# A hybrid Conformer/RWKV-7 step: recurrence steps and square sums traced next to the low-rank and block products

## The chip, the cores and the metric

The kernel runs on one core of one Trainium2 chip. The metric is the device time of one launch in microseconds; the kernel before took 2652.4 us, the median of three runs (2649.21, 2652.4 and 2652.9).

## The reference, cut to what matters

Two layers are applied to 1040 prompt tokens (16 learned ones and 1024 of the prompt) and to 8 single tokens that continue stored states. Layer 0 mixes with a causal convolution, layer 1 with RWKV-7; each is followed by a squared-ReLU MLP. The change touches layer 1's mixer alone:

```
r = xr @ w_r;  k = xk @ w_k;  v = xv @ w_v
w_log = -softplus(-(w0 + tanh(xw @ w1) @ w2)) - 0.5
decay = exp(-exp(w_log))
a = sigmoid(a0 + (xa @ a1) @ a2)
g = sigmoid(xg @ g1) @ g2
kk = k * k_k, divided by its norm in each head
k = k * (1 + (a - 1) * k_a)
# scan over tokens, S: 64 x 64 in each of 16 heads
sa = S @ -kk_t
S = S * w_t + outer(sa, kk_t * a_t) + outer(v_t, k_t)
y = S @ r_t
bonus = sum(r * k * r_k) * v
out = ((groupnorm(y) + bonus) * g) @ w_o
```

The scan over single tokens is computed in 17 chunks (16 tokens, then 16 times 64) with products of small matrices and the inverse of a triangular matrix in each chunk.

## The kernel before, in words

**Stages.** Layer 0 comes first, then layer 1's mixer input (about 1000 to 1715 us of the profiled execution), then layer 1's output projection, its MLP and the last norm. In the mixer input the tokens go through in four groups (`G1`, 272, 256, 256 and 264 columns; called group 0 to 3 here), and within a group in eight blocks `p` of 128 channels. The tokens of groups 0 to 3 make chunks 0 to 4, 5 to 8, 9 to 12 and 13 to 16.

**One block `p` of a group** (`mixer_in`) traces these products for TensorE, in this order: the `r` projection (`proj`, eight 128x128 weight blocks, tile `pr`); for p over 2 one block of the next group's `k` projection (`keys`, tile `pk`); the low-rank products `l_g` (full array) and `l_w`, `l_a` (64 rows of the array each, side by side); the `v` projection (`pv`); then for the block before it (`finish`, whose `trace` is called one block late through `late`) the transposes `vt`, the block products `nn` (64x32 parts of the array) and the bonus sum `pk<-rk`; and at last `pb`, which spreads the key norms. ScalarE takes `l_w` and `l_a` through two tanh and two copies (L1131, L1132), then `am`, `em` and `ex` (L1159, L1146, L1150); VectorE scans the decay (L1143) and makes the chunk's operands `ab`.

**The square sums.** Each block of `k` is squared on ScalarE (`sq`, L948) and its per-head sums are four products into the tile `pn` (L939, 128x32 parts of the array). Before the change those of a block follow the next `k` block's projection (`add_pn`).

**The recurrence** trails one group behind. `tick` lets it advance: `advance` adds `PACE` (1.4, 1.3, 2.4 in groups 1 to 3) to a credit and runs pieces of the generator `chunk` while the credit is positive; each piece costs its entry of `RW`. A chunk's pieces are: the products `A` in two halves (`front`, tiles `A`, 64x128 parts), `gg` (32x32 parts) with the transposes `bT`, `W` (128x64) with `po` (32x32), `U` (64x64), and `S` with `Y` (128x64). `norm_gate` adds transposes `yn`. `invert` advances the triangular inverses, which are VectorE work with a DMA on either side. Before the change a block calls `tick` five times through `both`: ahead of `r`, twice inside `r` (after weight blocks 2 and 5 of 8, `proj`'s `fill`) and twice inside `v`; a `k` block calls it twice more.

**What sets the order.** TensorE's order is the order of tracing (`tc.manual_schedule`). The other engines' orders are made by a scheduler from the dependencies, so they move when TensorE's order does. PSUM has four banks for the projections and the like (tag `mm`, used in turn), three for the recurrence (tag `w`) and one for `pn` (tag `x`). A product that needs a bank waits until what was in it has been read.

Of the kernel before, what the change touches and what calls it, by code (L numbers as in the profile page):

```python
# [8 lines left out]
F32 = mybir.dt.float32  # L9
# [7 lines left out]
P = 128  # L17
# [16 lines left out]
N1 = 272  # L34
# [12 lines left out]
def hybrid_step(tc, x_prompt, x_sample, state_conv, state_shift, state_wkv, meta_tokens,  # L47
# [10 lines left out]
    with ctx:  # L58
# [48 lines left out]
        for name, ap in vecs:  # L107
            n = ap.shape[0]
# [85 lines left out]
        def bank(name, tag="mm"):  # L194
            return cur[tag].tile([P, 512], F32, name=name, tag=tag)
# [200 lines left out]
        with ExitStack() as l0:  # L396
# [294 lines left out]
            with ExitStack() as s:  # L691
# [3 lines left out]
                fill, rest = filler(8 * KT, ([ranked(CV0, conv(0)), ranked(CV0, ln_silu(0))], EARLY * (15 * KT // 2 + 2 + 2 * MW + KT)))  # L695
# [4 lines left out]
                first = pw1_weights(0, 0)  # L700
# [5 lines left out]
                for g in range(3):  # L706
# [6 lines left out]
                    def both():  # L713
                        if g:
                            fill()
                        if g < 2:
                            nxt()
# [37 lines left out]
        for i, op in enumerate((ALU.is_gt, ALU.is_ge)):  # L755
            v = m_ar[:HS, i * HS:(i + 1) * HS]
# [75 lines left out]
        pr = pool(ld, "pr", 1)  # L832
# [86 lines left out]
        def proj(w, act, n, name, fill=None):  # L919
            ps = bank(f"p{name}")  # L920
            for k in range(KT):
                nc.tensor.matmul(ps[:, :n], w[:, k, :], act[k], start=k == 0, stop=k == KT - 1)  # L922
                if fill and k in (2, 5):
                    fill()
            return ps

        def keys(g, fill):

            c0, n = G1[g]
            nm = lambda s, *a: f"{s}{g}" + "".join(f"_{x}" for x in a)  # L930
            mix, _, act = prep[g]
            act = act or [mix(2, k) for k in range(KT)]
            pn = bank(nm("pn"), "x")
            add_pn = lambda: None

            def to_pn(p, sq):
                def add():
                    for j in range(4):
                        nc.tensor.matmul(pn[32 * j:32 * j + 32, :n // 4], head_sel(p), sq[:, n // 4 * j:n // 4 * (j + 1)],  # L939
                                         start=p == 0, stop=p == KT - 1, tile_position=(0, 32 * j))  # L940
                return add
            for p in range(KT):
                yield
                ps = proj(next(wrkv), act, n, nm("k", p), fill)
                k_ = kept[g, p] = pr.tile([P, N1], F32, name=nm("st", p), tag="st", bufs=KT + 1)
                nc.scalar.copy(k_[:, :n], ps[:, :n])
                sq = pr.tile([P, N1], F32, name=nm("sq", p), tag="rk", bufs=2)
                nc.scalar.activation(sq[:, :n], ps[:, :n], AF.Square, scale=vec("k_k", p))  # L948
                add_pn()
                add_pn = to_pn(p, sq)  # L950
            yield
            w = n // 4
            r16, low = (lorap.tile([P, N1 // 4], F32, name=nm("r16" + q), tag="lf", bufs=2)[:, :w] for q in "fl")
            high = lorap.tile([P, N1 // 4], F32R, name=nm("r16h"), tag="lh")[:, :w]
            norm[g] = lorap.tile([P, N1], F32R, name=nm("r16"), tag="r16", bufs=2)[:, :n]
            add_pn()
            nc.vector.tensor_scalar(r16, pn[:, :w], L2_EPS * L2_EPS, None, op0=ALU.max)
            nc.scalar.activation(r16, r16, AF.Sqrt)
            nc.vector.reciprocal(r16, r16)
# [7 lines left out]
        def mixer_in(g, tick):  # L967
# [63 lines left out]
            def t_(name, p, tag=None, bufs=1):  # L1031
                return pr.tile([P, N1], F32, name=nm(name, p), tag=tag or name, bufs=bufs)
# [19 lines left out]
                next(kend, None)  # L1052

            def finish(p, rk, ab, vv):
                def trace():
                    for s in segs:
                        if s[3] == HS:
                            nc.gpsimd.dma_start(d_ab[s[0], :, p].rearrange("c r i x -> r c (i x)"),
# [38 lines left out]
                    nc.gpsimd.dma_start(d_n[ch0:ch0 + ncg, p].rearrange("c r t -> r c t"), n32[:, :ncg])  # L1097
                    if g == 0:
                        nc.gpsimd.dma_start(d_n[0, p], n32[:, 4])
                    pb = bank(nm("pk", p))  # L1100
                    nc.tensor.matmul(pb[:, :n], hsum, rk[:, :n], start=True, stop=True)
                    bv = t_("bv", p)
# [1 line left out]
                    return lambda: nc.gpsimd.dma_start(d_bv[:, p, c0:c0 + n], bv[:, :n])  # L1104
                return trace

            late, later = (lambda: lambda: None), lambda: None
            for p in range(KT):
                both()
                ps = proj(next(wrkv), act, n, nm("r", p), both if p else first)  # L1110
                rk2 = pr.tile([P, 2, N1], F32, name=nm("rk2", p), tag="rk2", bufs=2)
                nc.scalar.copy(rk2[:, 1, :n], ps[:, :n])
                if p == 0:
# [13 lines left out]
                pls = [bank(nm("l2", f"{b}{p}")) for b in "wa"]  # L1127
                for i, pl in enumerate(pls):
                    nc.tensor.matmul(pl[:, :n], wa2[HALF[i], p, :], lwa[HALF[i], :n], start=True, stop=True, tile_position=(HS * i, 0))
                for pl, t, nb, sign in zip(pls, (cum, nav), ("w0", "a0"), (0.5, -0.5)):  # L1130
                    nc.scalar.activation(t[:, :n], pl[:, :n], AF.Tanh, scale=0.5, bias=hvec(nb, p))  # L1131
                    nc.scalar.activation(t[:, :n], t[:, :n], AF.Copy, scale=sign, bias=sign)  # L1132
                ps = proj(next(wrkv), act_v, n, nm("v", p), both)
                vv = t_("vv", p, "vv", 2)
                nc.scalar.copy(vv[:, :n], ps[:, :n])
                later()
                later = late()
                nkk, rp = (rk2[:, i, :] for i in range(2))
                kp = kept.pop((g, p))
                pb = bank(nm("pb", p))  # L1140
# [20 lines left out]
                bb, km = wa[:, 0, :], wa[:, 1, :]  # L1161
                nc.vector.tensor_mul(km[:, :n], kp[:, :n], am[:, :n])
                nc.vector.tensor_mul(bb[:, :n], nkk[:, :n], nav[:, :n])
                rk = t_("rk", p, "rk", 2)
                nc.vector.scalar_tensor_tensor(rk[:, :n], rp[:, :n], vec("r_k", p), km[:, :n], op0=ALU.mult, op1=ALU.mult)

                ab = pr.tile([P, 5, 4, HS], F32, name=nm("ab", p), tag="ab", bufs=2)
# [28 lines left out]

            def tail():
                later()
                late()()
                for c, k in ([(0, 1)] if g == 0 else []) + [(ch0, ncg)]:  # L1200
                    invs.append(inverses(c, k))
            carry["tail"] = tail
# [585 lines left out]
```

## Time and profile before

| | us |
|---|---|
| median of three runs | 2652.4 |
| the profiled execution | 2651.75 |
| its span, first to last instruction | 2649.8 |
| outside the span | 1.95 |
| TensorE busy in the span | 2594.1 |
| mean granted TensorE clock | 0.994 |

In the timeline of TensorE a row is a run of equal products: its start, its length up to the modelled end of the last one, and how many passes there are (an f32 product makes two). Since products overlap, the time that a run takes is the distance from its start to the next row's start. In front of the shapes stands the part of the array that the product uses, rows by columns: 128\*128 is all of it. Square brackets hold idle time in front of the row, with what ended it.

### The profile page before, as it was taken

How to read it: one execution, taken by the hardware profiler on the slowest of the kernel's cores; microseconds unless marked ns; L12 is line 12 of the kernel's file. 1: busy time of each engine (PE TensorE's matmuls, PEld its weight loads, DVE VectorE, ACT ScalarE, POOL GpSimd, SP SyncE). 2: the span in 40 equal slices, each digit the busy share in tenths (PEclk: the TensorE clock that was granted, in tenths of full speed). 3: DMA queues.
4: the chain of work that ended last, by engine and by line, in shares of the span. 5: the costliest groups of instructions: out<-in, count | busy, mean ns of one | idle time of the engine just before them, and what ended most of it. 6: DMA issues, size and time to landing. Idle time of an engine off the chain costs nothing.

```text
span 2649.8 us, 51719 instructions
## 1 busy us (share of the span) xinstructions
PE 2594.1 (98%) x19956; PEld 2432.9 (92%) x19956; DVE 1717.6 (65%) x3610; ACT 1128.8 (43%) x2093; POOL 1456.7 (55%) x2060
## 2 busy tenths in 40 slices
PE   9999999999999999999999999899999999999998
PEld 8999999999999999777777777789999999999998
DVE  6999999997444444445757567686679554444435
ACT  5546435444444333243344545545444542222223
POOL 7677878878878777022211113476588763333331
PEclk9999999999999999999999999999999999999999
DMA  7663544554446543677776867898575542222211
GB/s 190 172 168 108 167 141 133 160 172 137 138 138 187 155 136 112 191 211 202 214 184 181 213 160 194 218 207 195 142 219 174 153 132 65 72 68 69 72 48 44
DMA packets 602060, 400.24 MB, mean 151 GB/s; under 512 B 96128, under 2 KB 548928, under 8 KB 601814
## 3 DMA queue, kind: packets, MB, share of 16 engines
q1 hardware_dynamic: 573764, 360.08, 49.6%
q0 software_dynamic: 8720, 26.35, 3.0%
q10 hardware_dynamic: 19330, 10.49, 1.4%
q8 instruction: 158, 2.59, 0.4%
q14 instruction: 88, 0.72, 0.1%
HBM read 338.94 MB, written 58.83 MB: 150 GB/s over the span
## 4 chain that ended last, share of the span: by engine, by line
PE 85%; DVE 8%; ACT 2%; issue 2%; DMA 1%; POOL 1%; SPq 0%; ACTq 0%; DVEq 0%; POOLq 0%
PE ps_in L190 8%; PE ps_in L192 8%; PE ps_in L191 8%; PE out L190 8%; PE out L191 8%; PE out L192 8%; PE pk L922 4%; PE pr L922 4%; PE pv L922 3%; PE ps_g L190 1%; PE ps_o L192 1%; PE ps_g L191 1%; PE ps_g L192 1%; PE ps_oo L190 1%; PE ps_o L190 1%
## 5 line engine op out<-in xcount | busy, mean ns | idle before, releaser
L165 POOL TENSOR_TENSOR wo_lo<-wo_raw,wo_hi 128x256 fp32r<-128x256 f32 x736 | 543.0, 770 | 286.6 <-ACT wo_hi L158 279.2
L165 POOL TENSOR_TENSOR wi_lo<-wi_raw,wi_hi 128x256 fp32r<-128x256 f32 x640 | 474.5, 774 | 238.3 <-ACT wi_hi L158 237.9
L190 PE MATMUL out<-hh,wo_hi 128*128 128x352 f32 (+2 forms) x1536 | 497.5, 324 | 8.1 <-DVE h L360 6.5
L360 DVE TENSOR_TENSOR h<-h,out 128x352 f32<-128x352 f32 (+2 forms) x768 | 386.9, 512 | 168.2 <-PE out L192 166.6
L190 PE MATMUL ps_in<-m_h,wi_hi 128*128 128x352 f32 (+2 forms) x1536 | 494.0, 322 | 0.0
L192 PE MATMUL ps_in<-m_l,wi_hi 128*128 128x352 f32 (+2 forms) x1536 | 492.8, 321 | 0.7 <-DVE m_l L288 0.7
L191 PE MATMUL out<-hh,wo_lo 128*128 128x352 f32 (+2 forms) x1536 | 492.5, 321 | 0.0
L191 PE MATMUL ps_in<-m_h,wi_lo 128*128 128x352 f32 (+2 forms) x1536 | 491.5, 320 | 0.0
L192 PE MATMUL out<-hl,wo_hi 128*128 128x352 f32 (+2 forms) x1536 | 490.8, 320 | 0.0
L542 DVE SCALAR_TENSOR_TENSOR cv<-u,wdw,cv 128x348 f32<-128x348 f32 (+2 forms) x720 | 378.8, 577 | 0.7
L158 ACT CAST wi_hi<-wi_raw 128x1024 fp32r<-128x1024 f32 x160 | 167.6, 1049 | 383.7 <-PE out L192 191.1
L158 ACT CAST wo_hi<-wo_raw 128x1024 fp32r<-128x1024 f32 x184 | 192.7, 1048 | 313.0 <-PE out L192 167.1
L190 PEld LDWEIGHTS out<-hh,wo_hi 128*128 128x128 f32 x1536 | 289.1, 188 | 13.7 <-DVE h L360 9.0
L190 PEld LDWEIGHTS ps_in<-m_h,wi_hi 128*128 128x128 f32 x1536 | 289.2, 188 | 1.4
L192 PEld LDWEIGHTS ps_in<-m_l,wi_hi 128*128 128x128 f32 x1536 | 288.2, 188 | 2.0 <-DVE m_l L288 1.5
L191 PEld LDWEIGHTS out<-hh,wo_lo 128*128 128x128 f32 x1536 | 288.5, 188 | 0.8
L191 PEld LDWEIGHTS ps_in<-m_h,wi_lo 128*128 128x128 f32 x1536 | 288.5, 188 | 0.6
L192 PEld LDWEIGHTS out<-hl,wo_hi 128*128 128x128 f32 x1536 | 288.3, 188 | 0.0
L347 DVE SCALAR_TENSOR_TENSOR ps_in<-ps_in,rs_m 128x352 f32<-128x352 f32 (+2 forms) x192 | 100.7, 525 | 256.5 <-PE ps_in L192 256.1
L142 DVE TENSOR_TENSOR hl<-ps_in,hh 128x352 fp32r<-128x352 f32 (+2 forms) x192 | 98.9, 515 | 124.0 <-ACT hh L141 123.9
L1097 POOL DMA_DIRECT2D d_n<-n x32 | 24.5, 764 | 220.4 <-DVE n L1087 130.8
L348 ACT ACTIVATE ps_in<-ps_in 128x352 f32<-128x352 f32 (+2 forms) x192 | 85.1, 444 | 129.4 <-DVE ps_in L347 129.2
(371 smaller groups left out, 4734.5 us busy)
## 6 DMA issues: line engine op xcount, KB each, us to landing
wi_raw<-in_w_mlp_in_dram SPq DMA_DIRECT2D x160, 512.0 KB
wo_raw<-in_w_mlp_out_dram SPq DMA_DIRECT2D x160, 512.0 KB
wk_raw<-in_rwkv_w_k_dram SPq DMA_DIRECT2D x32, 512.0 KB
wr_raw<-in_rwkv_w_r_dram SPq DMA_DIRECT2D x32, 512.0 KB
wv_raw<-in_rwkv_w_v_dram SPq DMA_DIRECT2D x32, 512.0 KB
d_ab<-ab POOLq DMA_DIRECT2D x32, 512.0 KB, 4.3
pg_raw<-in_conv_w_pw_dram SPq DMA_DIRECT2D x24, 512.0 KB
pa_raw<-in_conv_w_pw_dram SPq DMA_DIRECT2D x24, 512.0 KB
```

What stands on the lines that cost most here:

```text
L142: return eng_lo.tensor_sub(lo, src, hi.bitcast(F32))
L158: cast = nc.scalar.copy(hi[:, :a * b], raw[:, :a * b])
L165: eng_lo.tensor_sub(lo[:, cs], raw[:, cs], hi[:, cs].bitcast(F32))
L190: nc.tensor.matmul(ps, w[0], act[0], start=first, stop=False)
L191: nc.tensor.matmul(ps, w[1], act[0], start=False, stop=False)
L192: nc.tensor.matmul(ps, w[0], act[1], start=False, stop=last)
L347: nc.vector.scalar_tensor_tensor(s, s, 0.0, rs()[:, :n], op0=ALU.max, op1=ALU.mult)
L348: nc.scalar.activation(s, s, AF.Square)
L360: total = nc.vector.tensor_add(hv[:, 4 * i + m, :], hv[:, 4 * i + m, :], ps[:, :n])
L542: nc.vector.scalar_tensor_tensor(acc[m][:, :n], ug[:, m, j:j + n], wdw[:, m, j:j + 1], acc[m][:, :n], op0=ALU.mult, op1=ALU.add)
L922: nc.tensor.matmul(ps[:, :n], w[:, k, :], act[k], start=k == 0, stop=k == KT - 1)
L1097: nc.gpsimd.dma_start(d_n[ch0:ch0 + ncg, p].rearrange("c r t -> r c t"), n32[:, :ncg])
```

## The change

The five calls of `both` in a block go to two places: three stand together right behind `l_w` and `l_a` (one in the first block of groups 1 to 3), and two stand in `trace`, behind `nn` and ahead of the bonus sum. The `r` and `v` projections hold none any more (in the first block of a group `r` keeps `first`); the `k` blocks keep theirs. The square sums wait in a list, `sums`, and are traced right behind `l_w` and `l_a` too, now of the `k` block that this block `p` has just projected; in a `k` block whatever is left over is traced ahead of the next square. The buffers under the tag `rk` go from two to three. The number of products and of calls of `both` stays.

```diff
+        sums = []
...
-            add_pn = lambda: None
...
                 nc.scalar.copy(k_[:, :n], ps[:, :n])
-                sq = pr.tile([P, N1], F32, name=nm("sq", p), tag="rk", bufs=2)
+                while len(sums) > (p == 1 and g > 0):
+                    sums.pop(0)()
+                sq = pr.tile([P, N1], F32, name=nm("sq", p), tag="rk", bufs=3)
                 nc.scalar.activation(sq[:, :n], ps[:, :n], AF.Square, scale=vec("k_k", p))
-                add_pn()
-                add_pn = to_pn(p, sq)
+                sums.append(to_pn(p, sq))
             yield
...
-            add_pn()
+            sums.pop(0)()
...
-                def trace():
+                def trace(fill):
...
                         nc.gpsimd.dma_start(d_n[0, p], n32[:, 4])
+                    fill()
+                    fill()
                     pb = bank(nm("pk", p))
...
-            late, later = (lambda: lambda: None), lambda: None
+            def none_yet(fill):
+                fill()
+                fill()
+                return lambda: None
+            late, later = none_yet, lambda: None
             for p in range(KT):
-                both()
-                ps = proj(next(wrkv), act, n, nm("r", p), both if p else first)
+                ps = proj(next(wrkv), act, n, nm("r", p), None if p else first)
...
                     nc.tensor.matmul(pl[:, :n], wa2[HALF[i], p, :], lwa[HALF[i], :n], start=True, stop=True, tile_position=(HS * i, 0))
+                while sums:
+                    sums.pop(0)()
+                for _ in range(3 if p or g == 0 else 1):
+                    both()
...
-                ps = proj(next(wrkv), act_v, n, nm("v", p), both)
+                ps = proj(next(wrkv), act_v, n, nm("v", p))
...
-                later = late()
+                later = late(both)
...
-                rk = t_("rk", p, "rk", 2)
+                rk = t_("rk", p, "rk", 3)
...
-                late()()
+                late(lambda: None)()
```

The first place is TensorE in group 1, block 6, where chunk 1 reaches `W` and `po` (`pk_4` is the fourth `k` block of the next group, `pv_6` this block's `v` projection). Before:

```order
L922 MATMUL pk_4_14823<-mx_2_2_14015,wk_4_raw 128x256
L1350 MATMUL W_14827<-sv,xa_12366 64x64 x16
L1325 MATMUL po_14849<-p_14573,gg_14735 32x32 x16
L922 MATMUL pk_4_14823<-mx_2_3_14018,wk_4_raw 128x256
L922 MATMUL pk_4_14823<-mx_2_4_14021,wk_4_raw 128x256
L922 MATMUL pk_4_14823<-mx_2_5_14024,wk_4_raw 128x256
L922 MATMUL pk_4_14823<-mx_2_6_14027,wk_4_raw 128x256
L922 MATMUL pk_4_14823<-mx_2_7_14030,wk_4_raw 128x256
L939 MATMUL pn_14032<-sq_3_14689,hsel 32x64 x4
L1028 MATMUL l_g_14891<-lg_13661,wg_12353 128x256
L1129 MATMUL l_w_14897<-lwa,wa_12355 128x256
L1129 MATMUL l_a_14898<-lwa,wa_12355 128x256
```

And after the change:

```order
L922 MATMUL pk_4_14827<-mx_2_7_14030,wk_4_raw 128x256
L1028 MATMUL l_g_14840<-lg_13661,wg_12353 128x256
L1134 MATMUL l_w_14846<-lwa,wa_12355 128x256
L1134 MATMUL l_a_14847<-lwa,wa_12355 128x256
L938 MATMUL pn_14032<-sq_4_14838,hsel 32x64 x4
L1359 MATMUL W_14854<-sv,xa_12366 64x64 x16
L1334 MATMUL po_14876<-p_14609,gg_14771 32x32 x16
L922 MATMUL pv_6_14911<-mx_3_0_13762,wv_6_raw 128x256
```

`W`, `po` and `pn` left the middle and the end of the `k` block and stand with `l_w` and `l_a`; `pn` takes the squares of `k` block 4 where it took those of block 3.

The second place is TensorE in group 1, block 5, between the first half of chunk 1's `A` (`A_14640`, `A_14641`; after the change `A_14677`, `A_14678`) and the second half. Before:

```order
L1274 MATMUL A_14641<-xa_12366,bk_14567 128x128
L922 MATMUL pr_5_14631<-mx_0_6_13713,wr_5_raw 128x256
L922 MATMUL pr_5_14631<-mx_0_7_13715,wr_5_raw 128x256
L922 MATMUL pk_3_14662<-mx_2_0_14009,wk_3_raw 128x256
L922 MATMUL pk_3_14662<-mx_2_1_14012,wk_3_raw 128x256
L922 MATMUL pk_3_14662<-mx_2_2_14015,wk_3_raw 128x256
L922 MATMUL pk_3_14662<-mx_2_3_14018,wk_3_raw 128x256
L922 MATMUL pk_3_14662<-mx_2_4_14021,wk_3_raw 128x256
L922 MATMUL pk_3_14662<-mx_2_5_14024,wk_3_raw 128x256
L1274 MATMUL A_14669<-xa_12366,bk_14567 128x128
L1274 MATMUL A_14670<-xa_12366,bk_14567 128x128
```

And after the change (the last of eight rows of the first half, and the first of the second):

```order
L1283 MATMUL A_14677<-xa_12366,bk_14603 128x128
L1283 MATMUL A_14678<-xa_12366,bk_14603 128x128
L1283 MATMUL A_14693<-xa_12366,bk_14603 128x128
L1283 MATMUL A_14694<-xa_12366,bk_14603 128x128
L1283 MATMUL A_14693<-xa_12366,bk_14603 128x128
```

The eight projection products between the halves are gone; the second half follows the first at once.

The third place is ScalarE at the same point after the change (`no` is a copy out of an `A` bank, `wa` are the tanh and copies of `l_w` and `l_a`):

```order
L1127 COPY gt_5_14663<-l_g_14661 128x256
L1140 ACTIVATE wa_5_14666<-l_w_14667,half 128x256
L1128 DMA d_g<-gt_5_14663 128x256
L1141 ACTIVATE wa_5_14666<-wa_5_14666 128x256
L1140 ACTIVATE wa_5_14666<-l_a_14668,half 128x256
L1141 ACTIVATE wa_5_14666<-wa_5_14666 128x256
L1155 ACTIVATE em_5_14798<-wa_5_14666 128x256
L1159 ACTIVATE ex_5_14800<-wa_5_14666 128x4x64
L1168 ACTIVATE wa_5_14666<-wa_5_14666,omka,negs 128x256
L1288 COPY no_14608<-A_14677 32x128
L1288 COPY no_14608<-A_14678 32x128
```

Before the change the two copies of the first half stood ahead of the block's `rk` copy, its `gt` and its tanh; now they stand behind the whole row of decay operations.

## The prediction

> **What bounds the kernel now.** The summary of the span comes first, then the table of windows over the mixer input of layer 1, the only stage whose order the change touches.
>
> ```profile
> span 2649.8 us, 51719 instructions
> PE 2594.1 (98%) x19956; PEld 2432.9 (92%) x19956; DVE 1717.6 (65%) x3610; ACT 1128.8 (43%) x2093; POOL 1456.7 (55%) x2060
> 1160.00:1715.00 555.00, 528.93 (x5733) 419.32 (x5731) 351.08 (x860) 250.55 (x644) 127.05 (x231) 0.99 0.75 195
> ```
>
> The last row has the stretch, its length, the busy time of TensorE, weight load, VectorE, ScalarE and GpSimd, the granted clock, the DMA share and the GB/s. TensorE is busy for 529 of 555 us and the next engine, VectorE, for 351. So the stage lasts as long as TensorE's row of products, and what can be won is of two kinds: the 26 us in which TensorE is idle, and time inside its busy rows that is not work. For the second kind the timeline of TensorE in group 1 is read, row start against row start.
>
> ```profile
> 1339.34 1.67 PE L922 MATMUL pr<-mx,wr_raw 128*128 128x256 f32 x7
> 1340.85 1.46 PE L922 MATMUL pk<-mx,wk_raw 128*128 128x256 f32 x6
> 1342.23 1.15 PE L1350 MATMUL W<-sv,xa 128*64 128x64 f32 x32
> 1343.32 0.69 PE L1325 MATMUL po<-p,gg 32*32 32x32 f32 x32
> ...
> 1347.81 2.86 PE L922 MATMUL pv<-mx,wv_raw 128*128 128x256 f32 x12
> 1350.59 1.15 PE L1366 MATMUL U<-w,p 64*64 64x64 f32 x32
> 1351.67 1.13 PE L922 MATMUL pv<-mx,wv_raw 128*128 128x256 f32 x4
> 1352.64 0.38 PE L1068 MATMUL vt<-ident,vv 128*128 128x128 f32 x2
> ...
> 1354.08 1.16 PE L1274 MATMUL A<-xa,bk 64*128 64x128 f32 x16
> 1355.17 2.86 PE L922 MATMUL pr<-mx,wr_raw 128*128 128x256 f32 x12
> 1357.96 1.15 PE L1377 MATMUL S<-uv,bkt 128*64 128x64 f32 x32
> 1358.94 1.10 PE L1384 MATMUL Y<-sv,xa 128*64 128x64 f32 x32
> 1359.88 1.10 PE L1386 MATMUL Y<-uv,nr 128*64 128x64 f32 x32
> 1360.91 1.13 PE L922 MATMUL pr<-mx,wr_raw 128*128 128x256 f32 x4
> 1361.88 0.38 PE L922 MATMUL pk<-mx,wk_raw 128*128 128x256 f32 x1
> ```
>
> Seven `pr` passes with full-array products on either side take 1.51 us (1339.34 to 1340.85), 0.216 us a pass. **The price of an excursion** from the full array into a small part is read against that:
> - The four `pr` passes from 1360.91 take 0.97 where 4 x 0.216 = 0.86, so 0.11 is paid behind a small product. The four `pv` passes from 1351.67 take 0.97 too.
> - The twelve `pr` passes from 1355.17 stand behind `A` and ahead of `S` and take 2.79, against 2.59: 0.20, of which 0.11 is the return from `A`, so 0.09 is paid ahead of a small product.
> - The 32 passes of `Y` from 1358.94, with the same part of the array on either side, take 0.94. The 32 from 1359.88, followed by the full array, take 1.03: 0.09 more. `S`, of the same shapes and behind the full array, takes 0.98: 0.04 more.
>
> Together an excursion costs 0.11 + 0.09 + 0.09 + 0.04 = 0.33 us. A step from one small part to another is cheaper: `W` with `po` behind it takes 1.09 (1342.23 to 1343.32) against `Y`'s 0.94, so I take 0.15.
>
> **The change part by part. Products and switches.** All 15,999 matrix products stay. In the whole order of TensorE's instructions, before and after, I counted where a product's part of the array differs from its predecessor's. Excursions that return to the full array go from 199 to 142, 57 fewer; steps from small to small go from 38 to 88, 50 more. (Most of the 57: 29 returns from the 64x128 part of `A`, `l_w` and `l_a`, 15 from `nn`'s 64x32, behind which a piece now often stands, 11 from `pn`'s 128x32.) The sum is -57 x 0.33 = -18.8, and +50 x 0.15 = +7.5: **-11.3 us**. Many of the 50 are pairs that the trace of before doesn't show, such as `A`'s part to `pn`'s. Below they are bounded by 0, where the next weights load unseen (-18.8 in all), above by a whole excursion's 0.33 (-2.3). I take 0.15 since `W` to `po` is the only such pair that the rows price.
>
> [...]
>
> **Square sums.** `pn` now needs the squares of the `k` block just ahead.
>
> ```profile
> 1346.68 0.47 ACT L948 ACTIVATE sq<-pk,pvec 128x256 f32<-128x256 f32 x1
> ...
> 1348.06 0.47 ACT L1131 ACTIVATE wa<-l_w,half 128x256 f32<-128x256 f32 x1 [0.40 <-PE l_a L1129]
> 1348.43 0.47 ACT L1131 ACTIVATE wa<-l_a,half 128x256 f32<-128x256 f32 x1
> 1348.79 0.72 ACT L1132 ACTIVATE wa<-wa 128x256 f32<-128x256 f32 x2
> 1349.54 0.60 ACT L1159 ACTIVATE wa<-wa,omka,negs 128x256 f32<-128x256 f32 x1
> 1350.05 0.40 ACT L1146 ACTIVATE em<-wa 128x256 f32<-128x256 f32 x1
> 1350.35 0.40 ACT L1150 ACTIVATE ex<-wa 128x256 f32<-128x256 f32 x1
> ```
>
> This is ScalarE at the same place. `sq` ends at 1347.15, and `l_g`, `l_w` and `l_a` cover it: TensorE leaves `l_a` at 1347.81, or some 0.3 earlier with `pn` gone from in front. Cost 0; without that cover it would be up to the 0.47 of `sq` in each of 21 blocks. The third `rk` buffer only lets `sq` live longer.
>
> **Waits that go.** The next rows are TensorE's waits for the copy of `pv` (`vv`) and the longest for `nr`, the masked `A`.
>
> ```profile
> PE pb L814 <- ACT vv L1135: 10.1, 8, 3.6
> ...
> 1278.90 0.58 PE L814 MATMUL pb<-r,hspread 128*128 128x256 f32 x1 [3.56 <-ACT vv L1135]
> 1427.21 0.39 PE L814 MATMUL pb<-r,hspread 128*128 128x256 f32 x1 [2.07 <-ACT vv L1135]
> 1441.66 0.39 PE L814 MATMUL pb<-r,hspread 128*128 128x256 f32 x1 [0.53 <-ACT vv L1135]
> 1658.24 0.39 PE L814 MATMUL pb<-r,hspread 128*128 128x264 f32 x1 [1.75 <-ACT vv L1135]
> 1591.30 0.52 PE L1343 MATMUL bT<-ident,bk 128*128 128x128 f32 x3 [3.20 <-DVE nr L1284]
> ```
>
> `pb` waits 10.1 us in eight places. Where one of the two ticks behind `nn` runs a piece, the wait is covered. In the new order no piece stands there at 1441.66 and 1658.24, so 0.53 and 1.75 stay; at 1278.90 it is one half of `A`, 1.09 us, so 2.47 stay. That leaves 10.1 - 0.53 - 1.75 - 2.47 = 5.35 to go. The 3.20 ahead of `bT` go as well, since `gg` and `bT` of that chunk move behind `pb`, the next `r` projection and `l_a`. Sum **-8.5 us**.
>
> **Waits that come.** The moved pieces stand right behind `l_w` and `l_a`, and so do, on ScalarE, the six operations of the decay quoted above. They end at 1350.75, 2.94 us after TensorE left `l_a`. What ScalarE or VectorE must do for a piece queues behind that, and the next piece follows at once where once half a projection lay between:
>
> ```profile
> L1279 ACT COPY no<-A 32x128 f32<-32x128 f32 x46 | 11.8, 256 | 27.1 <-PE A L1274 26.0 <-ACT vt L1070 0.4
> L1368 ACT COPY uv<-U 64x512 f32<-64x512 f32 x11 | 6.4, 581 | 29.1 <-DVE uv L1367 29.1
> L1282 DVE TENSOR_TENSOR xa<-A,m_ar 64x256 f32<-64x256 f32 x46 | 19.2, 417 | 6.1 <-ACT no L1279 5.5
> L1284 DVE TENSOR_TENSOR nr<-A,m_ar 128x256 f32<-128x256 f32 x46 | 19.1, 416 | 0.3
> ...
> PE Y L1384 <- DVE nr L1284: 1.9, 2, 1.5
> ```
>
> Three places are dear. In group 1, block 5, the two halves of chunk 1's `A` stand together and need four banks of three: the last waits for `no`, `xa` and `nr` of the first, 2.94 + 0.26 + 0.42 + 0.42 = 4.04 after `l_a`, less the 1.09 of the first half and 0.27 of the free bank: **2.7**. In group 2, block 7, half an `A`, `S` and `Y` stand together; the `Y` that reads `nr` waits 4.04 - 1.09 - 0.98 = **2.0**. In group 3, block 7, `U`, half an `A`, then `S`: it waits for `uv`, 2.94 + 0.58 less 1.08 and 1.09 = 1.35, up to 2.0 with VectorE's share of the copy; I take **1.9**. Five more in group 3 (the pairs `Y` and `A` in blocks 2 and 5, `po` and `U` in 3, `gg` and `W` in 1, `gg` and `bT` in 6) come to 0.9, 0.2, 0.45, 0.4 and 0.6, net of the 1.5 that `Y` waits in block 2 already. Sum **+9.2 us**. The bounds: 0, if the scheduler's rows are overtaken in time, and about 1.5 us in each of the 19 clusters in groups 1 to 3 that hold a piece, +28.
>
> **DMAs.** Of the moved ticks' transfers, SP's loads of `bk`, `xa`, `sv`, `uv` and `p` change places with one or two weight loads; POOL's stores of `d_n` keep their blocks. No wait of TensorE in this stage is for a projection's weights, so I take 0; the bound is the next block's load late once or twice, 2 us.
>
> **The clock.** It dips for 3.4 us behind two of the waits that go:
>
> ```profile
> 1428.00:1432.00 4.00, 4.00 (x13) 2.74 (x11) 4.00 (x12) 0.00 (x0) 1.82 (x4) 0.57 0.32 93
> 1592.00:1596.00 4.00, 4.00 (x13) 3.25 (x14) 3.93 (x11) 1.67 (x3) 3.04 (x4) 0.57 0.98 213
> ```
>
> At 0.57 in four microseconds each costs 1.7. They may go (-3.4), and the 2.7 us in front of `A` are long enough to bring one (+1.7), since 2.07 were enough at 1427. With the others' uncertain lengths I take 0.
>
> [...]
>
> **Sum:** -11.3 - 8.5 + 9.2 = -10.6, on 2651.75 for the profiled execution: 2641.2, rounded to **2641**. The median of the runs is 2652.4, 0.65 above that execution.
>
> **The rivals.**
> *Better: the new waits hardly come.* ScalarE is busy for 250 of 555 us, and the five small waits rest on 0.2 to 0.9 us. If only the three dear ones come at two thirds (4.4) and both dips go: -11.3 - 8.5 + 4.4 - 3.4 = -18.8, **2633**. Against it stands that each of the three is worked out from a fixed row.
>
> *Nothing is won: the switches cost elsewhere or the pairs are dear.* At 0.33 for each of the 50 new pairs the switches bring 2.3 instead of 11.3, and the waits balance: **2650**. This is also the case that the change doesn't do what it says, as a pair of small parts would then be two excursions. For it: most pairs are of kinds unseen before. Against it: `W` to `po`.
>
> *Slower: ScalarE's decay row becomes the bound of every cluster.* The mechanism is the one of block 5, at all 19. Without new waits 11.3 + 8.5 = 19.8 us are gained, so the mean wait at which the change turns is 19.8 / 19 = 1.04 us; slower by over 5.3 us it is from 1.32. My sum is 0.48 on average. At 1.5 it would be 2651.75 - 19.8 + 28.5 = **2660**. For it: the row of 2.94 us has no gap from 1348.06 on. Against it: in 11 clusters the next piece needs nothing from ScalarE, or a projection follows.
>
> **How the numbers follow.** My forecast has 0.58, the better case 0.18, nothing won 0.14, slower 0.10. A measurement of this kernel can tell about 0.2%, or 5.3 us, from no change. Forecast and better case are faster: 0.76; same 0.14; slower 0.10. The range: down to 2628 (the better case with pairs at 0.05), up to 2655 (nothing won, 2650.1, with 2 us for late loads, a dip of 1.7 and the 0.65 up to the median); some 0.08 is left out below, and 0.12 above.
>
> **What would show it.** In the profile after, `pv` should stand as one row of 16 passes of about 3.5 us, and `W`, `po` or `U` behind `l_a` with one return. The waits of `pb` for `vv` should add up to about 5 and the 3.20 of `bT` be gone. The new waits should be `A` and `Y` for `nr` (2.7 and 2.0) and `S` for `uv` (1.9), each with a ScalarE row that starts after `ex`. The forecast is wrong if a pair of small parts takes much over 0.15, if `pn` waits for `sq`, if `pb` waits as long for `vv` at its new place, or if the stage's mean clock falls.

## The result and the profile after

The change made the kernel slower by 0.16%: 2657.47 us against 2653.48 us, medians of 13 runs each, ratio 1.0016 with a 95% interval of 1.0009 to 1.0024. That lies outside the range of the prediction, and on the other side of before than 2641.

The summary of the span after, and the mixer input's row in the table of windows:

```profile
span 2654.6 us, 51711 instructions
PE 2587.1 (97%) x19956; PEld 2444.0 (92%) x19956; DVE 1716.0 (65%) x3610; ACT 1127.8 (42%) x2093; POOL 1455.3 (55%) x2060
...
1160.00:1715.00 555.00, 520.24 (x5684) 430.08 (x5682) 347.02 (x854) 248.62 (x638) 127.33 (x231) 0.97 0.74 195
```

TensorE has 7 us less busy time in the whole span, and the span is 4.8 us longer: work inside its rows became cheaper and idle time dearer. The mean clock of the stage fell from 0.99 to 0.97. TensorE's timeline in group 1, block 6, with what stood in pieces before:

```profile
1341.30 3.62 PE L922 MATMUL pr<-mx,wr_raw 128*128 128x256 f32 x16
1344.75 3.62 PE L922 MATMUL pk<-mx,wk_raw 128*128 128x256 f32 x16
...
1349.05 0.38 PE L1134 MATMUL l_w<-lwa,wa 64*128 64x256 f32 x1
1349.05 0.38 PE L1134 MATMUL l_a<-lwa,wa 64*128 64x256 f32 x1
1349.36 0.32 PE L938 MATMUL pn<-sq,hsel 128*32 128x64 f32 x8
1349.61 1.15 PE L1359 MATMUL W<-sv,xa 128*64 128x64 f32 x32
1350.69 0.69 PE L1334 MATMUL po<-p,gg 32*32 32x32 f32 x32
1351.31 3.72 PE L922 MATMUL pv<-mx,wv_raw 128*128 128x256 f32 x16
1354.87 0.38 PE L1068 MATMUL vt<-ident,vv 128*128 128x128 f32 x2
```

The projections are whole: `pv`'s 16 passes take 3.56 us (1351.31 to 1354.87), 16 x 0.216 and one return of 0.11. The last pass of `l_a` takes 0.31 ahead of `pn`, as it did ahead of the full array, so that this step by itself adds nothing; `W` with `po` behind it takes 1.08, against 1.09 before. TensorE's waits from 1180 to 1720 us, each row with total, number and longest:

```profile
PE A L1283 <- DVE nr L1293: 9.8, 3, 4.3
PE Y L1393 <- DVE nr L1293: 5.9, 3, 3.7
PE yn L1555 <- ACT uv L1377: 3.2, 1, 3.2
PE U L1375 <- ACT p L1368: 3.0, 1, 3.0
PE A L1283 <- issue: 2.7, 1, 2.7
PE U L1375 <- ACT ems L1513: 2.5, 1, 2.5
...
PE pb L814 <- ACT vv L1144: 1.6, 2, 1.4
PE S L1386 <- ACT uv L1377: 1.5, 1, 1.5
```

`pb`'s waits went from 10.1 to 1.6 us. Above them stands what took their place: recurrence pieces that wait for other engines' follow-on of the piece before.

**An account.** To put the terms side by side I took every profiled run from the first `r` product of the mixer to the first product of layer 1's MLP (6,625 recorded product starts in each) and went from start to start. What a step takes over the median step of its form in the kernel before is put down to switches (the two steps around a change of the used part, up to 0.33 us), to waits (steps longer by more than that), or to half clock (steps while the granted clock was 0.5). The rest is 565 us of plain products and 1 to 5 of small differences, in every run. The excursions are counted over more than the stretch: group 0's `k` blocks, ahead of it, are in them.

| kernel | excursions | switches | waits | half clock | stretch | measured against before |
|---|---|---|---|---|---|---|
| before | 199 | 45.1 | 29.9 | 12.7 | 656.9 | |
| the change | 142 | 32.4 | 40.7 | 17.4 | 658.5 | +0.16% |
| square sums only | 181 | 41.9 | 31.0 | 6.4 | 648.9 | -0.32% (-0.45 to -0.20) |
| three ticks behind `l_a` only | 176 | 40.6 | 48.2 | 15.9 | 672.2 | +0.60% (+0.47 to +0.73) |
| two ticks behind `nn` only | 183 | 42.4 | 25.9 | 12.3 | 648.3 | -0.37% (-0.49 to -0.24) |
| all ticks, no square sums | 160 | 36.6 | 39.5 | 19.0 | 662.0 | +0.10% (+0.01 to +0.19) |
| three ticks ahead of `l_w` | 143 | 31.3 | 34.9 | 8.2 | 642.5 | -0.39% (-0.52 to -0.27) |
| square sums and `nn` | 165 | 38.2 | 25.3 | 11.8 | 643.6 | -0.42% (-0.54 to -0.29) |
| square sums split | 283 | 72.9 | 30.6 | 9.9 | 681.0 | +1.51% (+1.37 to +1.65) |
| one tick behind `l_a` | 154 | 35.1 | 28.7 | 11.6 | 642.8 | -0.51% (-0.64 to -0.39) |
| one tick ahead of `l_w` | 155 | 33.4 | 28.1 | 15.0 | 643.8 | -0.52% (-0.65 to -0.40) |
| three ticks ahead of `r` | 160 | 35.8 | 34.0 | 17.6 | 654.6 | -0.05% (-0.14 to +0.03) |
| part that cost, ticks ahead | 177 | 37.9 | 41.6 | 12.9 | 660.9 | +0.07% (-0.02 to +0.16) |

The change: switches -12.7, waits +10.8, half clock +4.7. With the small differences the stretch is 1.6 us longer. A further 0.5 lies ahead of it and 2.7 behind it, where a dip of 3.4 us at 1951 that before does not have takes 1.7.

Two things limit this account. The division depends on the baseline: with a trimmed mean of the undisturbed steps in place of the median, the change has switches -14.6, waits +8.9 and half clock +6.1. The profile's own figures, which need no baseline, agree with it in size: TensorE's idle gaps in the stretch are 29.1 us before and 39.2 after, and half the time at a granted clock of 0.5 is 13.7 and 18.8. And each row is one execution, while the clock differs from one to the next: the profiled execution of the three ticks ahead of `l_w` has a mean clock of 0.995, its four others 0.992 or 0.993.

### The profile page after: what moved, and what is told of

It is laid out like the page before. It is cut to its first block, busy times and chain, and to the rows that moved or that the text cites. A ratio compares the mean times of both kernels' runs of the same rounds, so it can differ in the third digit from the quotient of the medians.

```text
span 2654.6 us, 51711 instructions
## 1 busy us (share of the span) xinstructions
PE 2587.1 (97%) x19956; PEld 2444.0 (92%) x19956; DVE 1716.0 (65%) x3610; ACT 1127.8 (42%) x2093; POOL 1455.3 (55%) x2060
## 4 chain that ended last, share of the span: by engine, by line
PE 84%; DVE 8%; issue 2%; ACT 2%; DMA 2%; POOL 1%; ACTq 0%; SPq 0%; DVEq 0%; POOLq 0%
PE ps_in L190 8%; PE ps_in L192 8%; PE ps_in L191 8%; PE out L190 8%; PE out L191 8%; PE out L192 8%; PE pk L922 4%; PE pr L922 3%; PE pv L922 3%; PE ps_g L190 1%; PE ps_o L192 1%; PE ps_g L191 1%; PE ps_g L192 1%; PE ps_oo L190 1%; PE ps_o L190 1%
## 5 line engine op out<-in xcount | busy, mean ns | idle before, releaser
L190 PEld LDWEIGHTS out<-hh,wo_hi 128*128 128x128 f32 x1536 | 289.7, 189 | 14.6 <-DVE h L360 9.9
```

Source lines behind the costliest of these rows:

```text
L190: nc.tensor.matmul(ps, w[0], act[0], start=first, stop=False)
```

## The experiments

Theory A was that the switches are worth their rows and that pieces placed behind `l_w` and `l_a` lose it again, since what they need stands behind ScalarE's decay row. Theory B: pieces side by side stall, wherever they stand. Theory C: the switches never were worth anything. 0.1% is 2.65 us here.

**One part alone.** `e1_sums` keeps the diff's lines on `sums` and puts the ticks back; `e3_nn` keeps `late(both)` with its two `fill()` and puts back the rest; `e2_low` and `e4_ticks` against the change:

```diff
e2_low, e4_ticks:
-                while len(sums) > (p == 1 and g > 0):
-                    sums.pop(0)()
...
-                sums.append(to_pn(p, sq))
+                add_pn()
+                add_pn = to_pn(p, sq)
...
-                while sums:
-                    sums.pop(0)()
e2_low:
-                fill()
-                fill()
                 return lambda: None
...
-                ps = proj(next(wrkv), act_v, n, nm("v", p))
+                ps = proj(next(wrkv), act_v, n, nm("v", p), both)
...
-                later = late(both)
+                later = late(lambda: None)
```

> Only the square sums move behind l_w and l_a; all ticks stay where they were before. In the order of TensorE's products that is 18 excursions fewer (199 to 181) and 15 more steps from small to small, all of them from l_a's part to pn's. Theory A (the switches are worth what the rows said, and the whole change lost it again to waits of pieces that stand side by side): 18 x 0.33 = -5.9 us, less nothing for the pairs, which took no extra time in the trace of the whole change: about -5 to -6 us against before, no new wait over 1 us. Theory C (the switches are hidden elsewhere and never were worth it): within 1.5 us of before.

> Only three ticks move, to behind l_w and l_a; v keeps its two, the square sums stay. 23 excursions fewer, 18 more small-to-small steps: -4.9 us by the rows. Theory A with the stalls bound to the place behind l_w and l_a (ScalarE's decay row): waits of A, Y, S, U for nr, uv and p of 8 us or more come here, and the clock dips behind them, so that this part is slower than before by 3 to 8 us. Theory B (what stalls is pieces side by side, wherever they stand): about the same as the part with the two ticks behind nn, -2 to +3 us in both.

> Only two ticks move, from inside v to behind nn; the other three and the square sums stay. 16 excursions fewer, 15 more small-to-small steps: -3.0 us by the rows. Theory A with the stalls bound to the place behind l_w and l_a: the waits of pb for vv are covered (-5 us or so) and few new ones come: -5 to -9 us. Theory B (pieces side by side stall anywhere): new waits of A and Y for nr of 4 us or more here too, -2 to +3 us.

> All five ticks move, the square sums stay: the change without its second half. 39 excursions fewer, 33 more small-to-small steps: -7.9 us by the rows. Theory A: the waits of the whole change come back, so it stands above the whole change by the 5 to 6 us that the square sums bring: +7 to +11 us against before. Theory C: like the whole change, +3 to +5. If the square sums cause part of the waits (a longer ScalarE queue at the cluster): below the whole change, 0 to +3.

Measured: 2645.65, 2670.61 and 2644.57 us, and 2658.64 for all ticks, with 2656.02 for before on the same chip. That is -8.5, +15.9, -9.8 and +2.7 us by the ratios. Theory C falls. The three ticks behind `l_w` and `l_a` cost 16 us by themselves, twice what theory A expected at most: switches -4.5, waits +18.3, half clock +3.2. The other two parts are faster. Of what the square sums won, only 3.2 us are switches, where 18 x 0.33 = 5.9 were expected: `l_a`'s last pass takes 0.31 ahead of `pn` and ahead of the full array alike, so a pair saves only the 0.09 into `pn`'s part and one return of 0.10. Another 6.3 are half clock in this execution; over all runs the mean clock is 0.9954 against 0.9939, some 4 us. All ticks without the square sums came out at +2.7, where theory A expected +7 to +11, and their interval overlaps that of the whole change: what the square sums win alone does not show inside it. The parts do not add up (-8.5 + 15.9 - 9.8 = -2.4, the whole +4): by the account they have switches -10.4, waits +15.4 and half clock -3.5 together, the whole -12.7, +10.8 and +4.7.

**The price of an excursion.** The kernel before, with each square sum's four products spread over the next `k` projection:

```diff
+                if parts and k in (0, 1, 3, 6):
+                    parts.pop(0)()
...
-                add_pn()
-                add_pn = to_pn(p, sq)
+                add_pn = to_pn(p, sq)
...
-                ps = proj(next(wrkv), act, n, nm("k", p), fill)
+                ps = proj(next(wrkv), act, n, nm("k", p), fill, add_pn)
```

> The price of an excursion by itself: the kernel before, with the four products of each square sum at four places inside the next k projection instead of together behind it. 84 excursions more (283 returns against 199), same products, and no wait of its own, since the squares are ready a block earlier. By the rows (0.09 into pn's part, 0.14 and 0.10 back): 84 x 0.33 = 28 us slower. If an excursion is hidden or was overestimated: under 15 us slower.

Measured: 2693.85 against 2653.57, +40 us. TensorE's timeline in one `k` projection of group 1:

```profile
1366.92 0.70 PE L922 MATMUL pk<-mx,wk_raw 128*128 128x256 f32 x2
1367.55 0.30 PE L940 MATMUL pn<-sq,hsel 128*32 128x64 f32 x2
1367.78 0.70 PE L922 MATMUL pk<-mx,wk_raw 128*128 128x256 f32 x2
```

Two passes and the step into `pn` take 0.63 (1366.92 to 1367.55) where 2 x 0.216 is 0.43, and `pn`'s two short passes with the way back 0.23. The four products together took 0.25 before (1346.30 to 1346.55): split up, they also stop overlapping. By the account an excursion into `pn`'s part costs 0.093 ahead, 0.142 behind and 0.104 at the return, 0.34 together, and another 0.07 is the lost overlap: 84 x 0.41 = 34 of the 40. Some of the rest are waits for `sq` in group 0, whose `k` blocks follow one another ahead of the stretch: 13 of the 40 us lie there. For this part of the array the term of the prediction stands.

**Behind or ahead.** The same three ticks on the other side of `l_w` and `l_a`, in the whole change (`e5_ahead`) and in the part that cost 16 us (`e16_low_ahead`):

```diff
+                for _ in range(3 if p or g == 0 else 1):
+                    both()
                 pls = [bank(nm("l2", f"{b}{p}")) for b in "wa"]
...
-                for _ in range(3 if p or g == 0 else 1):
-                    both()
```

> The whole change, but the three ticks of a block stand just ahead of l_w and l_a instead of just behind; l_w, l_a and the square sums follow them. 56 excursions fewer than before (143 against 199), 42 more small-to-small steps: the switches are worth about as much as in the whole change. Theory A (what costs is ScalarE's decay row, tanh to ex, that starts with l_w and l_a and stands ahead of what the pieces need): the copies no, uv and p now come ahead of that row, the waits of A, Y, S and U that the whole change has mostly go, and the time is 8 to 14 us under before. Theory B (what costs is three ticks in one place, whatever stands on ScalarE, since the next piece needs the one before it through VectorE and ScalarE): the waits stay within 5 us of the whole change's, and the time is 1 to 6 us over before.

> Three ticks just ahead of l_w and l_a, v keeps its two, the square sums stay: the part that cost 16 us alone, with its three ticks on the other side of l_w and l_a. Theory A: most of the 16 go, -4 to +4 us against before. Theory B (three in one place): +10 to +16, and what the whole change won by the same move came from its other parts.

Measured: 2642.38 against 2653.57 (-10.3 us by the ratio) and 2655.62 against 2653.45 (+1.9). Where it turned only this order, the same move was worth 14 us twice: from +4.2 to -10.3, and from +15.9 to +1.9. Theory B's form for one place does not survive that, since the three ticks are side by side in both. But theory A expected the waits to go for the most part, and by the account they give only 5.8 and 6.6 of the two 14s; half clock gives 9.2 and 3.0, the first in an execution with an unusually high clock, and in the second case switches give 2.7. What the order changes is seen at the two halves of `A` in group 1, block 5. ScalarE in the whole change, then TensorE:

```profile
1326.55 0.47 ACT L1140 ACTIVATE wa<-l_w,half 128x256 f32<-128x256 f32 x1
...
1327.86 0.42 ACT L1141 ACTIVATE wa<-wa 128x256 f32<-128x256 f32 x1
1328.22 0.42 ACT L1155 ACTIVATE em<-wa 128x256 f32<-128x256 f32 x1
1328.55 0.40 ACT L1159 ACTIVATE ex<-wa 128x256 f32<-128x256 f32 x1
1328.85 0.59 ACT L1168 ACTIVATE wa<-wa,omka,negs 128x256 f32<-128x256 f32 x1
1329.35 0.52 ACT L1288 COPY no<-A 32x128 f32<-32x128 f32 x2
```

```profile
1326.69 1.38 PE L1283 MATMUL A<-xa,bk 64*128 64x128 f32 x18
1330.94 1.44 PE L1283 MATMUL A<-xa,bk 64*128 64x128 f32 x10 [2.87 <-DVE nr L1293]
```

The first half of `A` is through by 1328.07, and its copies `no` start at 1329.35, when the decay row is done. VectorE takes `A` after that, and the second half stands 2.87 us; 2.7 was predicted. With the ticks ahead, ScalarE and TensorE at the same place:

```profile
1328.08 0.54 ACT L1288 COPY no<-A 32x128 f32<-32x128 f32 x2 [0.51 <-PE A L1283]
1330.36 0.54 ACT L1288 COPY no<-A 32x128 f32<-32x128 f32 x2 [1.74 <-PE A L1283]
1330.92 0.47 ACT L1140 ACTIVATE wa<-l_w,half 128x256 f32<-128x256 f32 x1
```

```profile
1326.89 1.38 PE L1283 MATMUL A<-xa,bk 64*128 64x128 f32 x18
1329.38 1.01 PE L1283 MATMUL A<-xa,bk 64*128 64x128 f32 x13 [1.11 <-DVE nr L1293]
```

`no` comes first and the decay row follows it; 1.11 are left. Not every wait hangs on this order: with the ticks ahead, 4.1 us at `A` (1281), 3.3 at `yn` (1443), 2.8 at `Y` (1603) and 2.7 at `A` (1657) remain.

**Three ticks elsewhere.** `e13_bunch_r` puts the same loop of three ahead of `proj(... nm("r", p) ...)`:

> The whole change with its three ticks together at the head of the block, ahead of the r projection, where no row of ScalarE operations of the same block starts. 39 excursions fewer than before, 35 more small-to-small steps: -7.7 us by the rows. Theory A (the place behind l_w and l_a costs): like the three ticks ahead of l_w and l_a, less the 17 excursions that come back (5.8): -4 to -10 us against before. Theory B (three ticks in one place cost, wherever): +3 to +10.

Measured: 2651.90 against 2653.45, -1.3 us: neither theory's number. The switches are worth 9.3 us there, and waits (+4.1) and half clock (+4.9) take them back. So three in one place also cost something away from `l_w`; theory A alone is too simple.

**Fewer ticks there, and the two good parts.** `e6_sums_nn` puts `both` back ahead of `r` and into it, `e9_one` leaves one tick behind `l_a`, `e12_one_ahead` one ahead of `l_w`:

```diff
e9_one:
-                ps = proj(next(wrkv), act, n, nm("r", p), None if p else first)
+                ps = proj(next(wrkv), act, n, nm("r", p), both if p else first)
...
-                for _ in range(3 if p or g == 0 else 1):
-                    both()
+                both()
```

> The square sums behind l_w and l_a and the two ticks of v behind nn; the other three ticks stay ahead of and inside r as before. These are the two parts that were faster alone (-8.5 and -9.8 us). 34 excursions fewer than before, 30 more small-to-small steps of which 15 (l_a to pn) took no extra time: -11.2 + 2.3 = -9 us of switches, and pb's waits covered. If the parts add up: -15 to -18 us against before. If both had won the same clock dips: -10 to -13.

> The whole change, but one tick behind l_w and l_a instead of three; the other two are inside r as before. 45 excursions fewer than before. If the loss goes with the number of ticks at that place (three alone there cost 16 us), one costs about 5: -8 to -12 us against before. If the loss needs two dependent pieces side by side, one tick costs next to nothing and saves switches: -16 to -21. If any piece behind l_w and l_a is late for ScalarE's row, whatever its neighbour: -3 to +3.

> The square sums, two ticks behind nn, one tick just ahead of l_w and l_a, two inside r as before. 44 excursions fewer than before, 35 more small-to-small steps. Against one tick behind l_w and l_a (-15 us) theory A, in which only the order on ScalarE counts, expects a little more, since the one piece is no longer behind the decay row: -15 to -20 against before. If a single piece there was never late, it is the same within 2 us.

Measured: 2642.69, 2638.61 (both with 2653.57 for before) and 2639.99 (2653.45): -11.1, -13.5 and -13.8 us. The two good parts add up in switches (-6.9; -3.2 and -2.7 alone) but not in half clock, where the square sums alone had won most. One tick behind `l_a` has 11 excursions fewer than none (-3.1 us in switches) for 3.4 us of waits; its -13.5 lies between the two first forecasts, and its interval overlaps that of no tick there. On which side of `l_w` it stands makes no difference, where theory A expected a little more from ahead. The two versions with one tick are faster than before by 0.5%. One tick as a rule is one piece, and the next follows a projection later.

**VectorE's inversion left out** of the change and of the kernel before (all row steps of the triangular inverse but the first are missing, so the scan's values differ):

```diff
-                with tc.issue_after(scans[group]) if j == top - 2 else nullcontext():
-                    nc.vector.tensor_mul(o, ...)
-                nc.vector.tensor_add(ni[:, :j, j + 1:top], ni[:, :j, j + 1:top], o)
+                if j == top - 2:
+                    with tc.issue_after(scans[group]):
+                        nc.vector.tensor_mul(o, ...)
+                    nc.vector.tensor_add(ni[:, :j, j + 1:top], ni[:, :j, j + 1:top], o)
```

> The whole change without the inversion of the triangular matrices on VectorE (all but the first of its row steps are left out, so the recurrence's values are not the reference's; all products, loads and stores stay). To be read beside the same cut in the kernel before, which runs on the same chip. Theory A1 (ScalarE's decay row is as dear as it is because its em waits for VectorE's scan, and the scan and the pieces' reads stand behind inversion steps): the whole change with the cut is 4 us or more under the kernel before with the cut, where it is 4 us over it without. Theory A2 (the row alone is enough): the two with the cut stay within 3 us of the distance that they have without it, +1 to +7.

> The kernel before without the inversion on VectorE (same cut, output not the reference's). TensorE is the bound and hardly ever waits for the inversion itself, so it should gain only what its waits for nr and vv owe to it: 0 to 8 us under before.

Measured: 2646.86 and 2644.42, with 2653.45 for before: the change stays 2.4 us behind where it was 4 behind. The waits of the change fall by 7.5 us and those of before by 5.6. VectorE's load makes waits longer in both kernels, and is not what sets them apart: theory A2's forecast. That the row on ScalarE is enough is not shown by this.

**One copy to VectorE.** `no` leaves ScalarE, in the change, in the kernel before and in the fastest version; the order on TensorE stays:

```diff
-                    nc.scalar.copy(no[Q[2 * q], js, :], pv[q][Q[2 * q], :, 32:64])
+                    nc.vector.tensor_copy(no[Q[2 * q], js, :], pv[q][Q[2 * q], :, 32:64])
```

> The whole change, with the small copy no (out of the bank of A) on VectorE instead of ScalarE. TensorE's order is that of the whole change to the last product; only one follow-on of A no longer stands behind ScalarE's decay row. Theory A (the decay row on ScalarE holds back xa, nr and with them the next piece): the waits of A and Y for nr shrink by 1 to 1.5 us each, some clock dips go with them, and the time is 5 to 10 us under the whole change, -1 to -6 against before. Rival (VectorE is as late as ScalarE, or the order on TensorE alone decides): within 3 us of the whole change, +1 to +7.

> The control: the kernel before with the copy no on VectorE. There only few pieces follow a piece at once, so little hangs on no: -4 to +2 us against before. If it gained as much as the whole change does by the same edit, the edit would say nothing about the place of the ticks.

> The fastest version so far (square sums and one tick behind l_w and l_a, two ticks behind nn, two inside r; -15 us) with the copy no on VectorE as well. Its waits of A for nr are 5.7 us and a dip follows the longest: -15 to -20 against before.

Measured: 2657.68, 2659.53 and 2650.55, with 2653.45 for before: the change as it was (+4.0 us against before), before slower by 5.8, the version with one tick some 10 us slower than it was. All three lie outside the ranges that went with theory A, and the first is what its rival expected. The edit costs 6 and 10 us in two kernels and nothing in the change. That difference would go with theory A, but a control that moves by more than the effect is no clean proof. The trace says more than the time: at the place of block 5, with TensorE's order unchanged, the second half of `A` now waits 1.32 us (1329.09) instead of 2.87, so the copy's place in ScalarE's queue made about half of that wait. In the whole list from 1180 to 1720, `A` and `Y` wait 4.1 us less for `nr`, and 2.3 us of new waits of `gg` for `no` and others stand against that.

## Why the prediction was wrong

**Switches: right.** Predicted -11.3 us, measured -12.7. An excursion into `pn`'s part costs 0.34, as four rows of the trace of before said of others. By the account the 50 new pairs cost 0.12 each on average, where 0.15 was taken. That this was so near is in part luck: the 15 pairs from `l_a` to `pn`, moved alone, came in the prediction's terms to 0.18 each (18 x 0.33 less the 3.2 measured), so that others must have cost less.

**Square sums: right.** Cost 0 predicted. Alone they brought one wait of 1.5 us for `sq`, in place of `pv`'s wait of 1.3 for it.

**Waits that go: right, and more.** `pb` keeps 1.6 us instead of the 4.75 predicted, and the 3.2 of `bT` shrank to 0.6.

**Waits that come: this step failed.** The three places that were worked out came nearly as said: 2.87 for 2.7, 1.6 for 2.0, 1.5 for 1.9. But together with the waits that go, the stretch should have changed by +0.7 and changed by +10.8. Missing were waits priced at next to nothing, or less than they became: 4.3 us at 1280 between two halves of `A`, the first behind `nn` and the second in a `k` block (2.47 of `pb` were expected to stay), 3.2 at `yn` (1447), 3.7 instead of 2.4 at `Y` (1610), 3.0 instead of 0.45 at `U` (1632), 2.7 between two halves of `A` that stand together behind `nn` at 1668, and 2.7 at `A` at 1714. Of these six only `Y` and `U` stand behind `l_w` and `l_a`. For such places I let ScalarE's row start when TensorE left `l_a` and last 2.94, from a block in which nothing else was in the way. At `Y` something was; first ScalarE, then TensorE:

```profile
1603.79 1.28 ACT L1140 ACT_TABLE_LOAD   x1 [0.44 <-PE l_w L1134]
```

```profile
1609.73 1.58 PE L1393 MATMUL Y<-sv,xa 128*64 128x64 f32 x30 [3.67 <-DVE nr L1293]
```

Here the decay row begins with the load of a table for the tanh, 1.28 us that the quoted block did not have, and VectorE was at inversion steps and the scan until 1608.7 before it took `A`. The 3.0 at `U` has another cause; again first ScalarE, then TensorE:

```profile
1626.53 0.38 ACT L1127 COPY gt<-l_g 128x264 f32<-128x264 f32 x1
1630.17 0.36 ACTq L1128 DMA_DIRECT2D d_g<-gt  x1
1630.63 0.48 ACT L1140 ACTIVATE wa<-l_w,half 128x264 f32<-128x264 f32 x1 [3.72 <-DMA bk<-d_ab]
...
1632.00 0.73 ACT L1368 COPY p<-po 32x256 f32<-32x256 f32 x2
```

```profile
1632.40 1.53 PE L1375 MATMUL U<-w,p 64*64 64x64 f32 x32 [2.96 <-ACT p L1368]
```

ScalarE stands from 1626.9 to 1630.2 at the issue of the store of `gt`, and tanh and `p` are queued behind it. The profile ends that stand with the landing of the load `bk`, which SP had issued at 1622.85 and which the store does not read. So by the profile a DMA made this wait, 3.72 us on ScalarE, and the 0 taken for DMAs was too small as well. In the old order half a projection, about 1.7 us (eight passes of 0.216), lay between a piece and the next, and by my estimate absorbed so much of such a delay, wherever it came from. I counted the cover only where I could see the delay.

**Clock: wrong by 4.7 us.** I took 0 for it; half clock rose from 12.7 to 17.4, and the dip at 1951 adds 1.7. This is not an accident of the two profiled executions: the mean granted clock is 0.9905 over the 13 runs of the change, and 0.9939 to 0.9947 over the sets of runs of the kernel before. The last section shows what the dips followed in these runs.

**The rivals.** The one that ended slower named the mechanism: pieces behind `l_a`, and ScalarE's row. Its condition, a mean wait over 1.04 us in all 19 clusters, was not met so evenly; fewer, longer waits did it, and several stood behind `nn` or in a `k` block. The waits and the clock together are +15.5 us where the forecast had +0.7, and that turns -12.7 into a loss.

**What stays open.** How much of the 14 us between behind and ahead is ScalarE's copies and how much VectorE's reads in their wake was separated at one place only, since moving `no` has its own price. Nor was it tried to move the decay row itself.

## What to carry to other kernels

Work placed side by side saved 12.7 us of switches on TensorE here and took away the cover of about 1.7 us that lay between dependent pieces; the waits grew by 10.8. So price each pair by the queue position of the copy between them on every engine, not by its duration: with `no` behind the decay row the next half of `A` waited 2.87 us, with `no` ahead of it 1.11. Before moving pieces next to a product, look at what that product starts on the other engines: ahead of it the same pieces were 14 us better here than behind it. Move one piece per place first: the version with one tick took 10.0 us of switches and had no more waits than the kernel before.

## What the runs showed of the hardware

In these runs half clock came on a fixed grid. Within each of the 18 profiled runs all dips start at whole multiples of 3.413 us from the first one (in the kernel before 44.0, 92.0, 128.0, 131.0 and 400.0 multiples behind the one at 1278.3, in the change 15.0, 49.0, 97.0, 104.0, 114.0, 127.0, 132.0, 197.0 and 401.0 behind the one at 1279.0), and those in the stretch last one to four of these steps. I cut the stretch into that grid and took the idle share of TensorE in each step that ran at full clock. Of 79 steps idle for over 55%, all were followed by a dip; of 35 idle for 45 to 55%, 21 were; of 50 idle for 35 to 45%, 2; of 3,109 idle for less, none. Before and the change alone, from 1065 to 1715 us, have 9 of 9, 1 of 3, none of 1 and none of 355. The ends of products are modelled, so the shares are good to a few per cent. Two windows of the kernel before, then three of the kernel with the square sums alone, cut on that grid:

```profile
1425.04:1428.46 3.42, 1.35 (x7) 1.06 (x7) 2.80 (x10) 2.38 (x6) 0.00 (x0) 1.00 1.06 184
1428.46:1431.87 3.41, 3.41 (x9) 2.31 (x7) 3.41 (x9) 0.00 (x0) 1.69 (x4) 0.50 0.33 98
```

```profile
1418.55:1421.97 3.42, 2.76 (x44) 1.92 (x42) 3.35 (x9) 2.38 (x5) 0.00 (x0) 1.00 0.71 148
1421.97:1425.38 3.41, 1.99 (x9) 1.72 (x10) 2.83 (x10) 1.63 (x5) 0.47 (x1) 1.00 0.85 200
1425.38:1428.79 3.41, 3.41 (x75) 2.89 (x74) 3.41 (x10) 0.51 (x2) 1.73 (x4) 1.00 0.25 62
```

It is the same wait of `pb`: 3.42 - 1.35 = 2.07 us idle in the first, 0.66 + 1.42 = 2.08 in the second. In the first it falls whole into one step (busy 1.35 of 3.42), and the next step has a clock of 0.50; in the second it is cut by a border (2.76 and 1.99 busy), and no dip follows. So by these windows a gap of 2 us costs 2 us or, with 1.7 (half of 3.41) for a dip of one step, 3.7, by where it falls; from this I estimate that a shift upstream that moves such a gap onto or off a border is worth 1.7 us for each gap. A part of the -0.32% of the square sums is this (6.3 us of half clock in the profiled execution).
